# GpSimd's long element-wise instructions in a streaming GLA and differential-attention step, issued as several short ones

## The chip, the cores and the metric

One core of one Trainium2 chip. The time is that of one launch of the kernel in microseconds of the device, the median of several runs. In the profile PE is TensorE's matmuls and PEld its weight loads, DVE is VectorE, ACT is ScalarE, POOL is GpSimd, and SP is the queue from which this kernel issues its DMAs. A name with a q behind it (SPq, POOLq) is an engine's sequencer, which issues in program order.

## What is computed

One layer of a streaming encoder for 1024 new frames of one stream (the "prompt") and 32 frames of a running one (the "sample"), model width 1024, all in 32-bit floats. A projection makes eleven pieces of the normed input; gated linear attention (GLA, 4 heads) and differential attention (8 heads) run beside each other; a merge joins them.

```python
u = rmsnorm(x, pre_norm_g) @ w_in          # split into gq gk gv gr gg dq dk dv dg ma mb
log_a = log_sigmoid(gr @ gla_w_a2 + gla_b_a) / 16
dq, dk = rope(dq, pos), rope(dk, pos)      # the first 16 of each half head's 64 columns
# GLA, in chunks of 64 frames, per head; b = cumsum(log_a)
o = (q * exp(b)) @ state + masked(q k^T exp(b_t - b_s)) @ v
state = exp(b_last) * state + (k * exp(b_last - b))^T @ v
# differential attention, per head, blockwise causal mask
attn = softmax(q1 k1^T / 8) - lam * softmax(q2 k2^T / 8)
o_diff = attn @ v
# merge
yg = rmsnorm(o_gla, gla_norm_g) * silu(gg)
yd = rmsnorm(o_diff, diff_subln_g) * (1 - lambda_init) * silu(dg)
merged = sigmoid(ma) * (yg @ w_proj_gla) + sigmoid(mb) * (yd @ w_proj_diff)
y = x + rmsnorm(merged @ w_out, post_norm_g)
```

The outputs are `y` for both streams, the rotated k rows, the v rows and the GLA states.

## The kernel before

Matmuls of full accuracy are built from pairs. Every operand is split into a high part, which is the number rounded to the matmul's type, and a low part, which is the number minus its high part; three matmuls then make a product (high by high, low weight by high, high weight by low). The splits cost one copy on ACT (the high part) and one subtraction on DVE or POOL (the low part).

The work runs in four stages. In the first (to some 225 us) the input is normed, split into `X` and multiplied with the value weights; the order of PE, ACT, DVE and POOL is written out by hand there. In the second (to some 570 us) the four GLA heads run, in the third (to some 1187 us) the eight heads of differential attention, and in the fourth the output projections and the merge. In the second and third stage a planner (`Order`) writes out PE's order ahead of time: it takes steps of the attention as they become due and fills the time between them with jobs of projection. The other engines' order comes from a scheduler.

A **fill job** multiplies all of `X` with one block of 128 columns of the input weights: three chunks of 352 frames, eight k-steps each, three matmuls a step (L461 `wh` by high, L462 `wl` by high, L463 `wh` by low). Its weights come from `wtile` (L424 to 432): a DMA loads `wr` (L427; there is one buffer of it), ACT makes `wh` (L429), POOL makes `wl` (L431, 128 partitions by 1024 columns, one instruction). They are asked for one job ahead. There are 72 such jobs. Since `wr` has one buffer, the load for the next job waits on SP until ACT and POOL have read the last one, and SP's later DMAs stand behind that load.

POOL also makes these: the low part of the GLA heads' values in `load_v` (L646, 128x512, five for each head, the fifth 32x256 for the sample); the product `sw * stb` of the rotation in `rot_job` (L796, 128x1056, for q and k of eight heads): `rr` is the projection, four DMAs (L794, L795) bring its rotated rows to `sw`, DVE multiplies `rr` with `ct` in three parts (L798) and adds `sw` in three parts (L800), and then `split_q` or `split_k` makes the pairs (L810 to L814, L829 to L832; DMAs at L835 bring k's halves to other partitions); the low part of the values of differential attention in `diff_main` (L909, 128x1024, one for each of eight heads); the power −1/2 in `rsqrt_mean` (L162), and small copies (L238, L847).

Lines of DVE that the prediction names: the scans of a GLA head's gates (L520), its q and k pairs (L540 to L545), its gated output (L718, which reads PSUM `ps_y`; SP stores the result to `ygd` at L721), the gating of a differential head (L861), the evacuations with SiLU (L474), the splits of attention weights (L930) and the sample's parts (L1005, L1021). L225 and L260 are stage 1's low parts of `X` and of the value weights, L213 the matmul that spreads the norm.

Of the kernel before, what the change touches and what calls it, by code (L numbers as in the profile page):

```python
# [11 lines left out]
F32 = mybir.dt.float32  # L12
# [3 lines left out]
ALU = mybir.AluOpType  # L16
# [9 lines left out]
KT = D // P  # L26
# [3 lines left out]
NQ = NP // P  # L30
# [92 lines left out]
def hybrid_step_kernel(ctx: ExitStack, tc: tile.TileContext, a):  # L123
    nc = tc.nc
# [6 lines left out]
    def pool(name, bufs=1, **kw):  # L131
        return tc.alloc_tile_pool(name=name, bufs=bufs, **kw)
# [12 lines left out]
    def tbank(name):  # L145
        return pp.tile([P, 512], F32, tag="t", name=name)

    def obank(name):
        return pp.tile([P, 512], F32, tag="o", name=name)
# [5 lines left out]
    ve.memset(eps, EPS)  # L155
    mhalf = cst.tile([P, 4], F32, name="mhalf")
    nc.gpsimd.memset(mhalf, -0.5)

    def rsqrt_mean(s, w, n, cnt):

        ve.tensor_scalar(s[0:w, 0:n], s[0:w, 0:n], 1.0 / cnt, EPS, op0=ALU.mult, op1=ALU.add)
        nc.gpsimd.tensor_tensor(s[0:w, 0:n], s[0:w, 0:n], mhalf[0:w, 0:n], op=ALU.pow)  # L162
# [262 lines left out]
    def wtile(b):  # L425
        wr = wp.tile([P, KT, P], F32, tag="wr", bufs=1, name="wr")
        dma(wr, a["w128"][b])  # L427
        wh = wp.tile([P, KT, P], F32R, tag="wh", name="wh")
        act(wh, wr, AF.Copy)  # L429
        wl = wp.tile([P, KT, P], F32R, tag="wl", name="wl")  # L430
        nc.gpsimd.tensor_tensor(wl, wr, wh.bitcast(F32), op=ALU.subtract)  # L431
        return wh, wl

    def proj(w, src, evac):
# [170 lines left out]
    def gla_head(h):  # L605
# [3 lines left out]
        for r, c in ((P, slice(0, 8)), (NS, slice(8, 9))):  # L609
            w = P if r == P else NS  # L610
# [27 lines left out]
        def load_v(pr):  # L638
            n, w = (2, P) if pr < 4 else (1, NS)
            vr = tp.tile([P, 2, GDV], F32, tag="vr", name="vr")  # L640
            vh = gp.tile([P, 2, GDV], F32R, tag="vh", bufs=2, name="vh")
            vl = gp.tile([P, 2, GDV], F32R, tag="vl", bufs=2, name="vl")
            dma(vr[0:w, 0:n, :], gvd[pr * 2 * P : pr * 2 * P + n * w, h * GDV : (h + 1) * GDV]
                .rearrange("(c p) e -> p c e", p=w))
            act(vh[0:w, 0:n], vr[0:w, 0:n], AF.Copy)  # L645
            nc.gpsimd.tensor_tensor(vl[0:w, 0:n], vr[0:w, 0:n], vh[0:w, 0:n].bitcast(F32), op=ALU.subtract)  # L646
            S.mark(("v", h, pr))
            vq[pr] = vh, vl

        load_v(4)  # L650
        for grp in (2, 0, 1):
            cs = range(grp * 4, grp * 4 + 4) if grp < 2 else range(8, 9)
            n, w = len(cs), P if grp < 2 else NS
# [12 lines left out]
            for c in cs:  # L666
# [5 lines left out]
                vh, vl = vq[c // 2]  # L672
                vh, vl = vh[0:w, c % 2, :], vl[0:w, c % 2, :]
# [86 lines left out]
    stb = dp.tile([P, T], F32, name="stb")  # L760
    dma(stb, a["ropes"])
    sw = dp.tile([P, T], F32, name="sw")
# [19 lines left out]
    def parts(n, cnt):  # L782

        return [slice(i * n // cnt, (i + 1) * n // cnt) for i in range(cnt)]
    SC = HD ** -0.5

    def rot_job(b, event, needs, split):
        def begin():
            r = dp.tile([P, T], F32, tag="rr", name="rr")

            def done():
                for m in range(2):
                    o = m * HD
                    dma(sw[o : o + 8], r[o + 8 : o + 16])  # L794
                    dma(sw[o + 8 : o + 16], r[o : o + 8])  # L795
                nc.gpsimd.tensor_tensor(sw, sw, stb, op=ALU.mult)  # L796
                for c in parts(T, N["rr"]):
                    ve.tensor_tensor(r[:, c], r[:, c], ct[:, c], op=ALU.mult)  # L798
                for c in parts(T, N["rr"]):
                    ve.tensor_tensor(r[:, c], r[:, c], sw[:, c], op=ALU.add)  # L800
                split(r)
            return (lambda ps, sl: act(r[:, sl], ps, AF.Copy)), done
        return b, event, begin, needs
# [47 lines left out]
    def diff_fin(h, osb, sqo):  # L851
        for n0 in (0, 512):
            yield 0.86, [(("pv", h, 3), W["pv"])], ["o"]
            ps = obank("ps_m")
            mm(ps, one_h, sqo[:, n0 : n0 + 512], start=True, stop=True)
            act(sqo[0:1, n0 : n0 + 512], ps[0:1], AF.Copy)
            S.free("o", W["m_o"])
        st(msd[h : h + 1, :], sqo[0:1, :])
        yield 0.0, [(("dg", h), 0.0)], []
        for c in parts(NP, N["fin"]):  # L860
            ve.scalar_tensor_tensor(osb[:, c], osb[:, c], gs_half, dsg[h][:, c], op0=ALU.mult, op1=ALU.mult)  # L861
        st(ydd[h, :, 0:NP], osb)
        S.mark(("fin", h))
# [32 lines left out]
    def diff_main():  # L896
        fin = None
        for h in range(DH):
            att = {}
            yield 0.0, [(("dq", h), 0.0), (("dk", h), 0.0)], []  # L900
            yield from diff_scores(h, 0, att)
            if fin is not None:
                yield from fin
            vr = tp.tile([P, NQ, P], F32, tag="sg1", name="vr")
            dma(vr, a["newv"][0:NP, h * P : h * P + P].rearrange("(c p) e -> p c e", p=P))
            vh = dp.tile([P, NQ, P], F32R, tag="vh", name="vh")
            vl = dp.tile([P, NQ, P], F32R, tag="vl", name="vl")
            act(vh, vr, AF.Copy)
            nc.gpsimd.tensor_tensor(vl, vr, vh.bitcast(F32), op=ALU.subtract)  # L909
            S.mark(("dv", h))  # L910
            osb = tp.tile([P, NP], F32, tag="o", name="osb")
            sqo = rp.tile([P, NP], F32, tag="gst", name="sqo")
            for i in range(NQ):
                g = i // 2
                if i + 1 < NQ:
                    yield from diff_scores(h, i + 1, att)
                p, lat = att.pop(i)
                if i % 2 == 0:
                    ah = dp.tile([P, NQ, 256], F32R, tag="ah", name="ah")
                    al = dp.tile([P, NQ, 256], F32R, tag="al", name="al")  # L920
                dsl = slice((i % 2) * P, (i % 2) * P + P)
                for j0 in range(0, i + 1, 4):
                    nj = min(4, i + 1 - j0)
                    yield 0.11 * nj, [(("p", h, i), lat)], ["t"]
                    ps = tbank("ps_t")
                    for j in range(j0, j0 + nj):
                        nc.tensor.transpose(ps[:, (j - j0) * P : (j - j0 + 1) * P], p[:, j * P : j * P + P], ident)  # L927
                    pv = ps[:, : nj * P].rearrange("p (c s) -> p c s", s=P)
                    act(ah[:, j0 : j0 + nj, dsl], pv, AF.Copy)  # L929
                    ve.tensor_tensor(al[:, j0 : j0 + nj, dsl], pv, ah[:, j0 : j0 + nj, dsl].bitcast(F32),  # L930
                                     op=ALU.subtract)
                    S.free("t", W["tr_t"])
                S.mark(("at", h, i))
                if i % 2 == 0:
                    continue
                yield 0.32 * (i + 0.5), [(("at", h, i), W["at"]), (("dv", h), W["dv"])], ["o"]
                po = obank("po")[:, 0:256]
                for j in range(i + 1):
                    cs = slice(0, 256) if j < i else slice(P, 256)
                    mm(po[:, cs], vh[:, j, :], ah[:, j, cs], start=(j == 0), stop=False)  # L940
                    mm(po[:, cs], vh[:, j, :], al[:, j, cs], start=False, stop=False)  # L941
                    mm(po[:, cs], vl[:, j, :], ah[:, j, cs], start=False, stop=(j == i))  # L942
                act(sqo[:, g * 256 : g * 256 + 256], po, AF.Square)
                act(osb[:, g * 256 : g * 256 + 256], po, AF.Copy)
                S.free("o", W["pv_o"])
                S.mark(("pv", h, g))
            fin = diff_fin(h, osb, sqo)
        yield from fin
# [85 lines left out]
    for h in range(-1, DH):  # L1034
        need = [(("qk", h - 1), 0.0)] if h >= 1 else []
        n = GATES_DIFF[h + 1]
# [8 lines left out]
    with tc.manual_schedule(engines=PE):  # L1045
        left = S.run(left + [[diff_main(), None, first], [sample_thread(), None, nullcontext],
                             [fill(jobs, xs), None, nullcontext]],
                     until=lambda: ("pv", DH - 1, 3) in S.at and jobs[-1][1] in S.at)
# [110 lines left out]
    for u in range(4):  # L1159
        wr = cp.tile([P, KT, 256], F32, tag="cwr", name="cwr")  # L1160
        dma(wr, a["wout"][u])
        if u == 0:
            wh = cp.tile([P, KT, 256], F32R, tag="cwh", name="cwh")
            wl = cp.tile([P, KT, 256], F32R, tag="cwl", name="cwl")
        else:
            wh, wl = (C[:, n, 0 : KT * 256].rearrange("p (k n) -> p k n", k=KT) for n in (2 * u - 2, 2 * u - 1))
# [6 lines left out]
    op = pool("op", reuse_waits="tile")  # L1173
# [6 lines left out]
    for u in range(4):  # L1180
        wh, wl = cw[u]
        csl = slice(u * 256, u * 256 + 256)
        for i in range(NQ + 1):
            t0 = i * P
            w = P if i < NQ else NS
# [111 lines left out]
```

## Time and profile before

| | |
|---|---|
| median of 3 runs | 1486.08 us (1483.74 to 1489.56) |
| the profiled execution's own time | 1489.96 us |
| its span | 1488.2 us |
| granted clock of TensorE, mean | 0.989 |
| PEld (weight loads) busy | 1330.4 us, 89% of the span |
| DVE busy | 790.4 us, 53% |
| ACT busy | 600.5 us, 40% |
| DMA traffic | 156.58 MB, 105 GB/s over the span |

A row of a timeline reads: start, duration (us from the start of the span), engine, line, operation, output from inputs, shape, count; in brackets how long the engine had been idle before it, and what ended that. A row of groups has the total busy time and the mean ns of one behind the first bar, then the idle time of the engine just ahead of such instructions with what ended it. A row of waits has the waiting engine and line, what it waited for, and then the total, the number of times and the longest. POOL is busy for a fifth of the span, in 186 instructions.

### The profile page before, as it was taken

The numbers are of one execution on the slowest core, as the hardware profiler recorded it, in microseconds if no ns is written. First come the engines' busy times: TensorE is split into PE (matmuls) and PEld (weight loads), VectorE is DVE, ScalarE is ACT, GpSimd is POOL, SyncE is SP. The second block draws the span as 40 slices with busy tenths as digits, with TensorE's granted clock in tenths as the row PEclk, the third lists the DMA queues.
The fourth block names the chain that finished last, engine by engine and source line by source line (L and its number), as shares of the span: only waits on it lengthen the run. The fifth ranks groups of instructions, "written<-read, shape, count | busy, mean of one in ns | idle before, by whom it ended". The sixth has DMA issues, their size and how long they took to land.

```text
span 1488.2 us, 22365 instructions
## 1 busy us (share of the span) xinstructions
PE 1427.6 (96%) x8848; PEld 1330.4 (89%) x8848; DVE 790.4 (53%) x1464; ACT 600.5 (40%) x1262; POOL 298.4 (20%) x186
## 2 busy tenths in 40 slices
PE   8999999998989999899999999999899899999997
PEld 6787778988989899899989998999799789999997
DVE  5612004565565443576767676768665536455415
ACT  4522114445444233355555555555454432221311
POOL 1200002132312133222222322222221111121001
PEclk9999999999999999999999999999999999999999
DMA  8621111122222134313141323233322278643205
GB/s 295 215 99 38 44 43 45 52 74 70 75 89 66 66 101 124 102 47 119 52 115 62 108 74 105 64 100 85 97 62 86 91 264 311 215 135 127 100 1 191
DMA packets 66742, 156.58 MB, mean 105 GB/s; under 512 B 10008, under 2 KB 28568, under 8 KB 65600
## 3 DMA queue, kind: packets, MB, share of 16 engines
q1 hardware_dynamic: 66624, 155.01, 32.2%
q8 instruction: 74, 1.21, 0.3%
q14 instruction: 44, 0.36, 0.1%
HBM read 104.39 MB, written 40.04 MB: 97 GB/s over the span
## 4 chain that ended last, share of the span: by engine, by line
PE 51%; DVE 5%; DMA 4%; ACT 2%; issue 1%; POOL 1%; SPq 0%; DVEq 0%; POOLq 0%; ACTq 0%
PE ps_w L461 9%; PE ps_w L462 9%; PE ps_w L463 9%; PE ps_w L440 2%; PE ps_w L439 2%; PE ps_w L441 2%; PE ps_c L1189 2%; PE ps_c L1191 2%; PE ps_c L1190 2%; PE ps_s L880 2%; PE ps_t L927 2%; PE ps_s L879 2%; DMA ydr<-ydd 1%; PE po L941 1%; PE po L942 1%
## 5 line engine op out<-in xcount | busy, mean ns | idle before, releaser
L461 PE MATMUL ps_w<-X,wh 128*128 128x352 f32 x1344 | 451.8, 336 | 8.4 <-ACT k L492 3.2
L462 PE MATMUL ps_w<-X,wl 128*128 128x352 f32 x1344 | 437.4, 325 | 0.0
L463 PE MATMUL ps_w<-X,wh 128*128 128x352 f32 x1344 | 435.5, 324 | 0.0
L431 POOL TENSOR_TENSOR wl<-wr,wh 128x1024 fp32r<-128x1024 f32 x72 | 178.5, 2479 | 659.6 <-ACT wh L429 535.9
L461 PEld LDWEIGHTS ps_w<-X,wh 128*128 128x128 f32 x1344 | 255.3, 190 | 13.5 <-issue 4.8
L462 PEld LDWEIGHTS ps_w<-X,wl 128*128 128x128 f32 x1344 | 255.3, 190 | 1.2 <-issue 1.2
L463 PEld LDWEIGHTS ps_w<-X,wh 128*128 128x128 f32 x1344 | 256.0, 190 | 0.0
L885 ACT ACTIVATE p<-ps_s,nm 128x256 f32<-128x256 f32 (+7 forms) x128 | 94.6, 741 | 58.7 <-DVE ps_s L881 31.0
L286 PE MATMUL ps_v<-wh,X 128*128 128x512 f32 x248 | 98.1, 396 | 1.9 <-DVE X L225 1.9
L285 PE MATMUL ps_v<-wh,X 128*128 128x512 f32 x248 | 99.5, 401 | 0.0
L287 PE MATMUL ps_v<-wl,X 128*128 128x512 f32 x248 | 98.9, 399 | 0.0
L429 ACT ACTIVATE wh<-wr 128x1024 fp32r<-128x1024 f32 x72 | 75.8, 1053 | 55.1 <-PE ps_w L463 30.4
L883 DVE TENSOR_REDUCE nm<-ps_s 128x1 f32<-128x256 f32 (+7 forms) x128 | 94.7, 746 | 2.7
L272 DVE TENSOR_TENSOR vo<-ps_v,vo 32x512 f32<-32x512 f32 x4 | 2.7, 678 | 141.7 <-ACT vo L271 141.7
L881 DVE MEMSET ps_s<- 64x64 f32 x128 | 14.3, 112 | 114.7 <-PE ps_s L880 113.1
L646 POOL TENSOR_TENSOR vl<-vr,vh 128x512 fp32r<-128x512 f32 (+1 forms) x20 | 24.8, 1238 | 223.9 <-ACT vh L645 223.9
L879 PE MATMUL ps_s<-k,q 128*128 128x512 f32 (+2 forms) x192 | 68.0, 362 | 1.2 <-DMA k<-k 1.2
L880 PE MATMUL ps_s<-kl,q 128*128 128x512 f32 (+2 forms) x192 | 63.9, 348 | 3.7 <-DMA kl<-kl 3.2
L268 ACT ACTIVATE vo<-ps_v 128x512 f32<-128x512 f32 x32 | 19.1, 596 | 116.5 <-PE ps_v L287 115.6
L929 ACT ACTIVATE ah<-ps_t 128x512 fp32r<-128x512 f32 (+2 forms) x96 | 46.9, 488 | 43.8 <-PE ps_t L927 43.1
L930 DVE TENSOR_TENSOR al<-ps_t,ah 128x512 fp32r<-128x512 f32 (+2 forms) x96 | 53.1, 553 | 18.7 <-ACT ah L929 17.4
L440 PE MATMUL ps_w<-Y,wl 128*128 128x352 f32 x192 | 62.3, 324 | 0.0
(319 smaller groups left out, 2971.0 us busy)
## 6 DMA issues: line engine op xcount, KB each, us to landing
wr<-w SPq DMA_DIRECT2D x72, 512.0 KB
thd<-gate SPq DMA_DIRECT2D x16, 528.0 KB
xn<-xn SPq DMA_DIRECT2D x16, 512.0 KB
wr<-wv SPq DMA_DIRECT2D x16, 512.0 KB
newk<-rr SPq DMA_DIRECT2D x8, 528.0 KB
ygr<-ygd SPq DMA_DIRECT2D x8, 528.0 KB
tha<-thd SPq DMA_DIRECT2D x8, 528.0 KB
ydr<-ydd SPq DMA_DIRECT2D x8, 528.0 KB
```

Of the source, the lines that this page charges most:

```text
L285: mm(ps, xk[:, 0, t0 : t0 + P], wh[:, k, :], start=(k == 0), stop=False)
L286: mm(ps, xk[:, 1, t0 : t0 + P], wh[:, k, :], start=False, stop=False)
L287: mm(ps, xk[:, 0, t0 : t0 + P], wl[:, k, :], start=False, stop=(k == KT - 1))
L431: nc.gpsimd.tensor_tensor(wl, wr, wh.bitcast(F32), op=ALU.subtract)
L440: mm(ps[:, :n], wl[:, k, :], src[k][:, 0, t0 : t0 + n], start=False, stop=False)
L461: mm(ps[:, :n], wh[:, k, :], src[k][:, 0, t0 : t0 + n], start=(k == 0), stop=False)
L462: mm(ps[:, :n], wl[:, k, :], src[k][:, 0, t0 : t0 + n], start=False, stop=False)
L463: mm(ps[:, :n], wh[:, k, :], src[k][:, 1, t0 : t0 + n], start=False, stop=(k == KT - 1))
L879: mm(ps[:, n0 : n0 + n], qs[m][:, qsl], ks[m][:, n0 : n0 + n], start=True, stop=False)
L880: mm(ps[:, n0 : n0 + n], qs[m][:, qsl], kls[m][:, n0 : n0 + n], start=False, stop=True)
L883: ve.tensor_reduce(nm, ps[:, 0:w], axis=AX.X, op=ALU.max, negate=True)
L885: act(p[:, 0:w], ps[:, 0:w], AF.Exp, bias=nm, accum_out=sm[:, m : m + 1])
```

## The change

A helper, `gp_tensor`, issues a `tensor_tensor` on POOL as `cnt` instructions, each on an equal share of the second dimension. Four places use it: `wl` in eight pieces of 128x128 (72 jobs), the value pairs of the GLA heads in two pieces of 128x256 (one for the sample's 32x256), the rotation's product in eight pieces of 128x132, and the value pairs of differential attention in eight pieces of 128x128. POOL's instructions grow by 688 (72 and 16 and 8 times seven, and 16 times one). What is computed stays the same.

```diff
+    def gp_tensor(out, in0, in1, op, cnt):
+
+        n = out.shape[1] // cnt
+        for i in range(cnt):
+            c = slice(i * n, i * n + n)
+            nc.gpsimd.tensor_tensor(out[:, c], in0[:, c], in1[:, c], op=op)
...
-        nc.gpsimd.tensor_tensor(wl, wr, wh.bitcast(F32), op=ALU.subtract)
+        gp_tensor(wl, wr, wh.bitcast(F32), ALU.subtract, KT)
...
-            nc.gpsimd.tensor_tensor(vl[0:w, 0:n], vr[0:w, 0:n], vh[0:w, 0:n].bitcast(F32), op=ALU.subtract)
+            gp_tensor(vl[0:w, 0:n], vr[0:w, 0:n], vh[0:w, 0:n].bitcast(F32), ALU.subtract, n)
...
-                nc.gpsimd.tensor_tensor(sw, sw, stb, op=ALU.mult)
+                gp_tensor(sw, sw, stb, ALU.mult, 8)
...
-            nc.gpsimd.tensor_tensor(vl, vr, vh.bitcast(F32), op=ALU.subtract)
+            gp_tensor(vl, vr, vh.bitcast(F32), ALU.subtract, NQ)
```

The order of instructions on PE, DVE, ACT and SP stays as it is; lines behind the helper are seven higher, and all pieces stand on the helper's line, L164. POOL's own order changes little beside the splitting. This is POOL around the branch of the third GLA head and behind it (`fl` is the flag of the branch, `ss` the norm of the head's sample rows); in the trace of before the `wl` behind the branch runs at 438.31. Before:

```order
L162 TENSOR_TENSOR ss<-ss,mhalf 128x4
L431 TENSOR_TENSOR wl<-wr,wh 128x1024 x2
L574 TENSOR_LOAD fl
L575 COMPARE_AND_BRANCH
L575 UNCONDITIONAL_BRANCH x2
L431 TENSOR_TENSOR wl<-wr,wh 128x1024
L646 TENSOR_TENSOR vl<-vr,vh 128x512
L162 TENSOR_TENSOR ss<-ss,mhalf 32x1
L431 TENSOR_TENSOR wl<-wr,wh 128x1024
```

The same place on POOL after the change:

```order
L169 TENSOR_TENSOR ss<-ss,mhalf 128x4
L164 TENSOR_TENSOR wl<-wr,wh 128x128 x14
L581 TENSOR_LOAD fl
L582 COMPARE_AND_BRANCH
L582 UNCONDITIONAL_BRANCH x2
L164 TENSOR_TENSOR wl<-wr,wh 128x128 x10
L164 TENSOR_TENSOR vl<-vr,vh 128x256 x2
L169 TENSOR_TENSOR ss<-ss,mhalf 32x1
L164 TENSOR_TENSOR wl<-wr,wh 128x128 x8
```

Each subtraction is a run of pieces, and the last two pieces of the `wl` ahead of the branch now stand behind it.

The second place is POOL in the third differential head, where the rotation's product, the weights and the values follow one another (`smp` and the 64x1 `ss` belong to the sample's rows); the values run at 750.74 in the trace of before. Before:

```order
L847 COPY smp<-sg 128x32
L431 TENSOR_TENSOR wl<-wr,wh 128x1024
L909 TENSOR_TENSOR vl<-vr,vh 128x1024
L431 TENSOR_TENSOR wl<-wr,wh 128x1024
L162 TENSOR_TENSOR ss<-ss,mhalf 64x1
L796 TENSOR_TENSOR sw<-sw,stb 128x1056
```

After the change POOL has there:

```order
L854 COPY smp<-sg 128x32
L164 TENSOR_TENSOR wl<-wr,wh 128x128 x8
L164 TENSOR_TENSOR vl<-vr,vh 128x128 x8
L164 TENSOR_TENSOR wl<-wr,wh 128x128 x8
L169 TENSOR_TENSOR ss<-ss,mhalf 64x1
L164 TENSOR_TENSOR sw<-sw,stb 128x132 x8
```

The sequence is the same, with eight instructions for each long one.

The third place is PE at the start of a fill job in the first GLA head, with the semaphores that each matmul waits for (`pf` belongs to the head's flag). Before:

```order
L525 MATMUL pf<-ident,fm 1x128 [waits DVE_49]
L461 MATMUL ps_w<-X_88,wh 128x352 [waits Activation_49]
L462 MATMUL ps_w<-X_88,wl 128x352 [waits Pool_49]
L463 MATMUL ps_w<-X_88,wh 128x352
L461 MATMUL ps_w<-X_88,wh 128x352
L462 MATMUL ps_w<-X_88,wl 128x352
L463 MATMUL ps_w<-X_88,wh 128x352
```

The same matmuls on PE after the change:

```order
L532 MATMUL pf<-ident,fm 1x128 [waits DVE_49]
L468 MATMUL ps_w<-X_88,wh 128x352 [waits Activation_49]
L469 MATMUL ps_w<-X_88,wl 128x352 [waits Pool_49]
L470 MATMUL ps_w<-X_88,wh 128x352
L468 MATMUL ps_w<-X_88,wh 128x352
L469 MATMUL ps_w<-X_88,wl 128x352 [waits Pool_49]
L470 MATMUL ps_w<-X_88,wh 128x352
```

In the first chunk each matmul on `wl` now waits for its own piece, where only the first one waited for all of it. PE's rows with a wait for POOL grow from 102 to 594.

## The prediction

> **What bounds the kernel now.** I read the page's busy line first.
>
> ```profile
> PE 1427.6 (96%) x8848; PEld 1330.4 (89%) x8848; DVE 790.4 (53%) x1464; ACT 600.5 (40%) x1262; POOL 298.4 (20%) x186
> ```
>
> The span is 1488.2 us, so PE stands idle for 1488.2 − 1427.6 = 60.6 us; the change leaves PE's own work alone, so all it can move lies in these 60.6. Next come PE's waits: engine and line, what ended the wait, then us in total, times, and the longest.
>
> ```profile
> PE ps_t L927 <- DVE al L930: 4.1, 3, 1.4
> PE ps_y L715 <- DVE yt L718: 3.9, 3, 2.6
> PE ps_st L1002 <- DVE smp L1005: 3.6, 2, 2.3
> PE ps_s L880 <- DMA kl<-kl: 3.2, 3, 2.2
> PE ps_w L461 <- ACT k L492: 3.2, 1, 3.2
> PE po L696 <- DVE o_sb L705: 3.1, 5, 0.9
> PE ps_w L461 <- DVE sg L474: 3.0, 2, 1.9
> PE ps_kt L629 <- DVE k L621: 2.1, 2, 1.3
> ...
> PE ps_n L213 <- POOL ssx L162: 1.8, 2, 1.3
> ```
>
> No row of the list waits for `wl` or for either `vl`: POOL's subtractions are not what PE waits for. Most rows name DVE. So the question is what POOL's long instructions do to DVE, and to the queues behind them. POOL's groups, with their mean ns behind the comma:
>
> ```profile
> L431 POOL TENSOR_TENSOR wl<-wr,wh 128x1024 fp32r<-128x1024 f32 x72 | 178.5, 2479 | 659.6 <-ACT wh L429 535.9 <-PE ps_t L927 55.8 <-ACTq L575 37.6
> L796 POOL TENSOR_TENSOR sw<-sw,stb 128x1056 f32<-128x1056 f32 x16 | 40.8, 2553 | 13.4 <-DMA sw<-rr 10.3 <-DVE sg L474 1.8 <-DVE sm L888 1.2
> L646 POOL TENSOR_TENSOR vl<-vr,vh 128x512 fp32r<-128x512 f32 x16 | 21.8, 1365 | 49.2 <-ACT vh L645 49.2
> ...
> L238 POOL CAST xsm<-X 128x64 fp32r<-128x64 f32 x8 | 1.5, 238 | 4.2 <-DVE X L225 4.2
> ```
>
> **The price of a piece.** No row shows a 128x128 subtraction on POOL. Its bounds come from the undisturbed medians (minimum/median/maximum ns) and from the one place where POOL runs eight short instructions in a row.
>
> ```profile
> L431 POOL TENSOR_TENSOR wl<-wr,wh x72: 2344/2403/3341, 25.2 to 1360.7; 128x1024 fp32r<-128x1024 f32 x72
> L646 POOL TENSOR_TENSOR vl<-vr,vh x20: 726/1292/1862, 230.8 to 542.2; 128x512 fp32r<-128x512 f32 x16, 32x256 fp32r<-32x256 f32 x4
> ...
> 65.77 1.49 POOL L238 CAST xsm<-X 128x64 fp32r<-128x64 f32 x8 [4.25 <-DVE X L225]
> ```
>
> (2403 − 1292) / 512 = 2.17 ns for each column, which leaves 2403 − 1024 × 2.17 = 181 ns fixed. A piece alone is 128 × 2.17 + 181 = 459 ns. The eight casts take 238 ns each but follow one another every (1.49 − 0.24) / 7 = 0.18 us, so 0.06 us of the fixed part overlaps. I take 0.40 us a piece, **3.3 us for eight** where one took 2.40: +0.9. The bounds are 2.40 (all of the fixed part overlaps: +0) and 8 × 0.459 = 3.67 (none: +1.27). The Trainium skill ("GPSIMD Engine Reference", section 3.1) gives 4497 ns for 2048 columns; by it the fixed part would be an estimated 53 ns, eight pieces some 2.65 us, and the sum below about 2 us lower. The trace's 181 ns disagrees and decides.
>
> Lateness of `wl` itself costs nothing: each is made one job ahead. The tightest place I found is this one, a subtraction and the first matmul on it:
>
> ```profile
> 1214.81 2.40 POOL L431 TENSOR_TENSOR wl<-wr,wh 128x1024 fp32r<-128x1024 f32 x1 [29.34 <-ACT wh L429]
> ...
> 1218.83 0.32 PE L462 MATMUL ps_w<-y,wl 128*128 128x352 f32 x1
> ```
>
> 1.62 us lie between; piece k is asked for only k × 0.48 us later, so +0.9 still fits, and so does +1.27. The added waits of PE, one for each piece, are then met before they are asked; I take 0 for them. A bound from above: all of PE's idle time, 60.6 us over 8848 matmuls, is 0.007 us each, so some 490 more waits are under 3.4 us.
>
> Three short runs change places on POOL: a power now stands between two halves of `vl`, six of eight pieces of one `wl` stand ahead of a branch and two behind it (twice), and a copy of `smp` stands inside a run of `wl`. Each moves something by at most a few pieces, 1 us, against a job of 72 matmuls at 1427.6 / 8848 = 0.16 us, 11.6 us, by which `wl` is ahead: 0; the bound is the 1.62 above.
>
> **What is gained: DVE gets in earlier.** These rows are of POOL and DVE at one place, and of the PE wait behind it.
>
> ```profile
> 438.31 2.51 POOL L431 TENSOR_TENSOR wl<-wr,wh 128x1024 fp32r<-128x1024 f32 x1 [14.54 <-ACT wh L429]
> 440.79 1.40 POOL L646 TENSOR_TENSOR vl<-vr,vh 128x512 fp32r<-128x512 f32 x1
> ...
> 438.56 2.55 DVE L520 TENSOR_TENSOR_SCAN b<-ones,t 128x128 f32<-128x128 f32 x1
> 441.03 1.45 DVE L520 TENSOR_TENSOR_SCAN b<-ones,t 128x128 f32<-128x128 f32 x1
> 446.38 0.43 PE L461 MATMUL ps_w<-X,wh 128*128 128x352 f32 x1 [1.90 <-DVE sg L474]
> ```
>
> A scan takes 0.4 us, but this one stands until 441.11, 0.29 us after POOL's instruction ends; the next one stands until 442.48, when POOL's second ends. Between POOL's two, the first scan did get in. So DVE is let in where one POOL instruction ends, even if the next is ready. With pieces, a held DVE instruction waits for a piece, not for eight. The four scans would alternate with pieces at some 0.5 us each and end near 440.6 instead of 442.8: 2.2 us earlier, more than PE's 1.9. Gain **1.9**. At the other places:
>
> ```profile
> L861 DVE SCALAR_TENSOR_TENSOR osb<-osb,gs_half,sg x8: 1286/2979/3004, 682.0 to 1188.1; 128x1024 f32<-128x1024 f32 x8
> L545 DVE TENSOR_TENSOR kl<-t,kh x4: 2098/2221/2231, 257.8 to 488.1; 128x1056 fp32r<-128x1056 f32 x4
> L543 DVE TENSOR_TENSOR t<-k,t x4: 1257/1258/1258, 255.4 to 485.6; 128x1056 f32<-128x1056 f32 x4
> ```
>
> - L861 takes 1.29 free and 2.98 at the median, held by POOL's `vl` (L909). It stands ahead of `smp` (L1005) in both L1002 waits (3.6 us, the shorter 1.3): 1.4 earlier each, capped by 1.3, gives **2.7**.
> - L545 takes 2.22 where L543 of the same size takes 1.26, held by `wl`. Two of its four stand ahead of L718 and a PE wait of 0.6 (3.9 − 2.6 over the other two): **1.2**.
> - L927, L492, L629 (4.1 + 3.2 + 2.1 us) and a few waits of 0.4 (0.8) sum to 10.2. Held DVE instructions are among those ahead of each, seldom the last one. I take a quarter, **2.6**; the bounds are 0 and 10.2.
>
> Sum of the gains: 8.4.
>
> **What is lost: what stands behind POOL's last piece.** SP's queue issues in order, and its load of the next weights waits until POOL has read the old ones:
>
> ```profile
> SPq L427 <- POOL wl L431: 187.2, 56, 14.7
> ...
> 387.25 2.51 POOL L431 TENSOR_TENSOR wl<-wr,wh 128x1024 fp32r<-128x1024 f32 x1 [4.50 <-ACT wh L429]
> 388.78 2.09 DVE L542 TENSOR_TENSOR ql<-t,qh 128x1056 fp32r<-128x1056 f32 x1
> 389.78 0.34 SPq L427 DMA_DIRECT2D wr<-w  x1
> 390.22 0.38 SPq L721 DMA_DIRECT2D ygd<-yt  x1
> 394.63 0.75 DVE L718 SCALAR_TENSOR_TENSOR yt<-ps_y,gg_half,sg 128x512 f32<-128x512 f32 x1 [1.73 <-DMA ygd<-yt]
> 396.10 0.38 PE L696 MATMUL po<-vh,ah 128*128 128x256 f32 x1 [0.86 <-DVE o_sb L705]
> ```
>
> The load goes out when POOL ends (389.76). The store of `ygd` behind it frees `yt`, L718 waits for that, and PE waits for the copy behind L718. After the change POOL needs 3.3 us, and L542 (I take 1.1 us by itself, a little under the 1.26 of L543, which is of its size), which today stands until POOL is done, gets in between two pieces and holds POOL in turn. POOL ends near 387.25 + 3.3 + 1.1 = 391.65: the store and PE are **1.9** later. Of the five waits at L696 in PE's list three stand behind such a store, one in each of three heads: 3 × 1.9 = 5.7. Bounds for one: 0.9 if DVE holds nothing up, 2.3 with the price at its upper bound.
>
> In stage 1 the chain `wl`, then the power for `ssx`, then the broadcast `ps_n` is on PE's path:
>
> ```profile
> 50.82 2.39 POOL L431 TENSOR_TENSOR wl<-wr,wh 128x1024 fp32r<-128x1024 f32 x1 [3.58 <-ACT wh L429]
> ...
> 54.51 1.46 POOL L162 TENSOR_TENSOR ssx<-ssx,mhalf 128x1 f32<-128x1 f32 x1 [1.29 <-DVE ssx L161]
> ...
> 56.02 0.58 PE L213 MATMUL ps_n<-ident,ssx 128*128 128x128 f32 x1 [0.52 <-POOL ssx L162]
> ```
>
> Eight pieces, with two DVE subtractions of 1.1 us together let in between, end near 55.2, and the power, behind a DVE instruction of 1.2, near 56.9 instead of 55.97: **1.0**. Losses: 6.7. Bounds: 3.0 and 8.
>
> **Sum.** −8.4 + 6.7 = −1.7 us. The profiled execution took 1489.96 (span 1488.2 and 1.76 around it); it would take 1488.3. It lies 3.9 above the median of three, 1486.08, within the runs' own spread of 1483.74 to 1489.56, and the sum is a difference, so I set it against the median: **1484.4**. A difference under 0.5% (7.4 us) is about what a measurement of this kernel can tell from none.
>
> **The rivals.** *The queue price isn't paid.* If POOL's pieces cost nothing extra and the stores behind them don't move, the 8.4 stand alone, and up to 7.6 more where I took a quarter: 1470 to 1478, near 1476. For it: 60.6 us of idle with DVE named in most rows. Against it: the in-order queue above. Chance 0.23.
>
> *The lock isn't given back between pieces.* A queued piece might take it again before DVE does. Then a held instruction waits 3.3 instead of 2.4 at nine places: 9 × 0.9 + 6.7 = +14.8, about 1501. The scan at 438.56 speaks against it, though it got in where POOL's next instruction was of another tile. Chance 0.06. The Trainium skill ("SBUF — State Buffer", section "Who interferes with whom") calls the shared port pair an exclusive lock, which the first to start holds; the trace agrees that DVE stands, 2.55 us for a scan of 0.4. It doesn't say who is next when pieces are queued; by a lock that queued pieces keep, it would be this rival.
>
> *The rotation becomes late (slower).* The product `sw` is on the way to k, and PE already waits for `kl` (3.2 us, three times).
>
> ```profile
> 914.73 2.44 POOL L796 TENSOR_TENSOR sw<-sw,stb 128x1056 f32<-128x1056 f32 x1
> ...
> 917.18 0.94 DVE L798 TENSOR_TENSOR rr<-rr,ct 128x352 f32<-128x352 f32 x2
> ```
>
> The additions (L800) come after three products with `ct` of 0.47, 1.4 us after `sw` ends here, so +0.9 is hidden. It decides from 1.4 on: at 0.46 a piece, with DVE's products let in between, `sw` takes 2.44 + 1.27 + 0.5 and eight heads pay up to 1.27 each: −1.7 + 10.2 = +8.5, about 1495. Chance 0.11.
>
> *It doesn't do what it says.* `load_v` is cut in two only, or one. If short pieces were merged on POOL, nothing would change: 1486. The order of instructions speaks against that: 0.03.
>
> **How the numbers follow.** The forecast has what is left, 0.57, and its own range is 1478.7 to 1490 (gains of 5.8 to 10.4 against losses of 3 to 8 give 1478.7 to 1488.3, and the runs' spread some 2 more above). The range of all is 1475 to 1497: it leaves out the far part of the first rival (0.08) and of the two slower ones (0.08). Faster 0.23; within 0.5% 0.57 + 0.03 = 0.60; slower 0.06 + 0.11 = 0.17.
>
> **What would show it.** Pieces 0.40 us apart, POOL busy for some 380 us instead of 298; scans at 438 of under 0.6 each and the 446.38 wait gone; L861 near 1.6; L696's wait over 5 us. I am wrong if a piece is under 0.33 or over 0.46 us, if DVE stands through more than one piece, or if `ygd` goes out as before.

## The result, and the profile after

The changed kernel takes **1503.74 us**, the median of four runs (1501.04 to 1505.80), where the kernel before takes 1486.00 (four runs, 1483.74 to 1489.56): a ratio of 1.0109, with a 95% interval of 1.0083 to 1.0135. The forecast of 1484.4, with its range of 1475 to 1497, was wrong, and in sign too. The profiled execution took 1504.61 us, with a span of 1502.9.

The page's line of busy times, of the kernel after:

```profile
PE 1434.4 (95%) x8848; PEld 1339.1 (89%) x8848; DVE 741.5 (49%) x1464; ACT 600.1 (40%) x1262; POOL 439.8 (29%) x874
```

PE's waits in the same kernel (total us, times, longest):

```profile
PE po L703 <- DVE o_sb L712: 10.3, 4, 3.3
PE ps_w L468 <- DVE tha L1085: 4.3, 5, 1.8
PE ps_a L561 <- DVE yt L725: 4.1, 2, 2.1
...
PE ps_w L468 <- DVE sg L481: 1.1, 1, 1.1
PE ps_st L1009 <- DVE smp L1012: 0.8, 1, 0.8
```

DVE is busy for 49 us less: it stands less behind POOL, as meant. The waits for `sg` (3.0 before) and `smp` (3.6 before) shrank as forecast. But the wait at `po` (L696 before, L703 now) grew from 3.1 to 10.3, and two rows are new or larger: `ps_a` for `yt`, and `ps_w` for `tha` (0.8 before). PE's busy time itself grew by 6.8 us.

Both traces hold the same 8848 matmuls in the same order, so the delay of each against its twin can be read off, and summed by the time in the trace of before:

| stretch of the kernel before | gained or lost after the change |
|---|---|
| 0 to 200 us (stage 1) | +0.4 |
| 200 to 300 (first GLA head) | −2.9 |
| 300 to 500 (GLA heads) | **+17.3** |
| 500 to 1050 (differential heads) | −6.0 |
| 1050 to 1200 | +0.7 |
| 1200 to 1300 (projections, merge) | **+3.8** |
| behind the last matmul | +1.4 |

The sum is the 14.7 us between the two spans. The medians lie 17.7 apart: the profiled execution of before took 4.0 us more than its median, that of after 0.9 more. This is the place in the GLA heads that the prediction worked out, from the timeline after: POOL's weights, DVE, SP, DVE, and PE.

```profile
390.90 4.73 POOL L164 TENSOR_TENSOR wl<-wr,wh 128x128 fp32r<-128x128 f32 x8 [3.79 <-ACT wh L436]
392.43 1.42 DVE L549 TENSOR_TENSOR ql<-t,qh 128x1056 fp32r<-128x1056 f32 x1
395.65 0.35 SPq L434 DMA_DIRECT2D wr<-w  x1
396.09 5.38 SPq L728 DMA_DIRECT2D ygd<-yt  x2
400.37 0.75 DVE L725 SCALAR_TENSOR_TENSOR yt<-ps_y,gg_half,sg 128x512 f32<-128x512 f32 x1 [4.35 <-DMA ygd<-yt]
401.85 0.58 PE L703 MATMUL po<-vh,ah 128*128 128x256 f32 x1 [3.23 <-DVE o_sb L712]
```

The chain is the forecast one. `wl` takes 4.73 us from its first piece to its last where it took 2.51. SP's load goes out when it ends, `ygd` behind the load, and PE stands for 3.23 us instead of 0.86. The next `wl` of the same head does it again, at a place that the prediction didn't look at:

```profile
412.59 4.53 POOL L164 TENSOR_TENSOR wl<-wr,wh 128x128 fp32r<-128x128 f32 x8 [2.56 <-ACT wh L436]
417.15 0.33 SPq L434 DMA_DIRECT2D wr<-w  x1
422.05 0.75 DVE L725 SCALAR_TENSOR_TENSOR yt<-ps_y,gg_half,sg 128x512 f32<-128x512 f32 x1 [5.84 <-DMA ygd<-yt]
422.86 0.33 PE L561 MATMUL ps_a<-qh,kh 128*128 128x128 f32 x1 [2.06 <-DVE yt L725]
```

The same place in the kernel before:

```profile
405.41 2.52 POOL L431 TENSOR_TENSOR wl<-wr,wh 128x1024 fp32r<-128x1024 f32 x1 [2.51 <-ACT wh L429]
407.96 0.33 SPq L427 DMA_DIRECT2D wr<-w  x1
409.74 3.75 SPq L721 DMA_DIRECT2D ygd<-yt  x2
```

There the load left 1.8 us ahead of the store of `ygd`, which waited for DVE alone. Now the load is what the store waits for.

In the merge it is the loads of `ydr` (L1062 before) that come late. These rows are again of the kernel after:

```profile
1266.28 4.40 POOL L164 TENSOR_TENSOR wl<-wr,wh 128x128 fp32r<-128x128 f32 x8 [9.42 <-ACT wh L436]
1270.70 0.33 SPq L434 DMA_DIRECT2D wr<-w  x1
1271.79 0.32 SPq L1143 DMA_DIRECT2D rsb<-rsd  x1
1272.96 1.92 SPq L1069 DMA_DIRECT2D ydr<-ydd  x2
1268.88 2.88 DVE L1144 TENSOR_TENSOR ydr<-ydr,rsb 128x1024 f32<-128x1024 f32 x2 [3.35 <-DMA ydr<-ydd]
1282.88 2.49 DVE L1144 TENSOR_TENSOR ydr<-ydr,rsb 128x1024 f32<-128x1024 f32 x2 [4.78 <-DMA ydr<-ydd]
1287.03 0.43 PE L468 MATMUL ps_w<-y,wh 128*128 128x352 f32 x1 [1.81 <-DVE tha L1085]
```

DVE's scaling waits 4.78 us for the loads of `ydr`, and DVE is late for PE. But the load of weights isn't what holds them at this place: it leaves 1.1 us ahead of SP's next instruction, `rsb`, and that one leaves 0.03 us after DVE's last scaling ended (1271.76). The loads of `ydr` are used 9.9 us after the first is issued (1272.96 to 1282.88), where 6.6 stood in the kernel before (1249.22 to 1255.85). Why they land later isn't shown by these rows.

Of the 17.3 us in the GLA heads only some 8.0 are changes of a wait by over 0.4 us. The rest is PE's pace. These are windows of PE: the stretch, its length, PE's busy time and count, and then the granted clock. The first six rows are of the kernel after.

```profile
325.50:333.50 8.00, 7.99 (x40) 0.57 0.33 99
326.45:333.27 6.82, 6.82 (x33) 0.50 0.25 76
343.51:346.93 3.42, 3.42 (x14) 0.50 0.21 77
401.54:404.95 3.41, 3.10 (x13) 0.50 0.52 154
486.87:490.29 3.42, 3.42 (x14) 0.50 0.55 153
507.35:514.18 6.83, 6.83 (x30) 0.50 0.10 38
```

And two of the kernel before; the first is the same work as the first row above:

```profile
326.00:334.00 8.00, 7.49 (x60) 1.00 0.37 115
...
506.40:509.80 3.40, 3.40 (x13) 0.50 0.50 157
```

The first row reaches a little past its stretch; cut to the stretches, the clock is one half, for 3.41 or 6.83 us: 40 matmuls in 8 us where 60 ran before. Half of the 23.9 us of the five stretches is 12.0; read by twins, their matmuls lost 10.7. Gaps that changed by less than 0.4 us give back 1.4, and the three make the 17.3. Four of the stretches stand behind waits that the change made longer (`po` three times, `ps_a` once). The one at 343.51 stands behind a wait of 2.65 us that the kernel before has too, at 340.51, and without a loss of clock there.

Outside these heads the kernel before has more of it: from 200 to 1450 us its stretches at half clock last 17.1 us and those of the kernel after 34.1, so 8.5 us were lost by the clock over the whole kernel. The mean clock of the other executions agrees: 0.980 to 0.984 in the four of the changed kernel, 0.988 to 0.995 in 52 of the kernel before.

### The profile page after: what moved, and what is told of

It is laid out like the page before. It is cut to its first block, busy times and chain, and to the rows that moved or that the text cites. A ratio compares the mean times of both kernels' runs of the same rounds, so it can differ in the third digit from the quotient of the medians.

```text
span 1502.9 us, 23109 instructions
## 1 busy us (share of the span) xinstructions
PE 1434.4 (95%) x8848; PEld 1339.1 (89%) x8848; DVE 741.5 (49%) x1464; ACT 600.1 (40%) x1262; POOL 439.8 (29%) x874
## 5 line engine op out<-in xcount | busy, mean ns | idle before, releaser
L164 POOL TENSOR_TENSOR wl<-wr,wh 128x128 fp32r<-128x128 f32 x576 | 278.5, 519 | 582.8 <-ACT wh L436 464.2
L164 POOL TENSOR_TENSOR vl<-vr,vh 128x128 fp32r<-128x128 f32 (+2 forms) x100 | 63.1, 661 | 244.0 <-ACT vh L652 219.1
L164 POOL TENSOR_TENSOR sw<-sw,stb 128x132 f32<-128x132 f32 x128 | 64.7, 540 | 2.7 <-DMA sw<-rr 1.9
L937 DVE TENSOR_TENSOR al<-ps_t,ah 128x512 fp32r<-128x512 f32 (+2 forms) x96 | 53.1, 553 | 18.7 <-ACT ah L936 17.3
```

The lines of the kernel that those rows point to most:

```text
L164: nc.gpsimd.tensor_tensor(out[:, c], in0[:, c], in1[:, c], op=op)
```

## The experiments

Two theories were set against each other at first. **Q**: the loss is `wl`'s later end, handed on by SP's order. **N**: the loss is the price of 688 more instructions and 492 more waits. A third, **R**, blames the rotation's product and the values.

**Only the weights in pieces** (`e1_only_wl`): the other three places whole.

```diff
-            gp_tensor(vl[0:w, 0:n], vr[0:w, 0:n], vh[0:w, 0:n].bitcast(F32), ALU.subtract, n)
+            nc.gpsimd.tensor_tensor(vl[0:w, 0:n], vr[0:w, 0:n], vh[0:w, 0:n].bitcast(F32), op=ALU.subtract)
...
-                gp_tensor(sw, sw, stb, ALU.mult, 8)
+                nc.gpsimd.tensor_tensor(sw, sw, stb, op=ALU.mult)
...
-            gp_tensor(vl, vr, vh.bitcast(F32), ALU.subtract, NQ)
+            nc.gpsimd.tensor_tensor(vl, vr, vh.bitcast(F32), op=ALU.subtract)
```

> Only the weights' subtraction (wl) is in eight pieces; the rotation's product and both value subtractions are whole again. Theory Q (SP's queue: wl ends 0.9 to 2.2 us later, the load of the next weights stands behind it on SP, and the ygd stores and ydr loads behind that; PE then stalls, and runs slowly after the longer stalls): the loss is nearly all here, 1500 to 1506 us, with three waits at the po matmuls of 3.3 us each and two at ps_a of 2.1 as in the changed kernel. Theory R (the loss comes from the rotation's product and the values in pieces): 1484 to 1490. Theory N (490 more waits on PE and 688 more instructions cost by their number): 504 of 688 are here, so about three quarters of the loss, 1499, spread evenly over the span and without those five waits.

Measured: 1505.39 us, ratio 1.0129 (1.0107 to 1.0152). The whole loss is here. Its waits for PE:

```profile
PE po L703 <- DVE o_sb L712: 10.5, 4, 3.5
PE ps_a L561 <- DVE yt L725: 4.1, 2, 2.1
PE ps_st L1009 <- DVE smp L1012: 3.6, 2, 2.3
```

The five long waits are those of the changed kernel, and the wait for `smp` is that of before. R is out.

**All but the weights in pieces** (`e2_all_but_wl`).

```diff
-        gp_tensor(wl, wr, wh.bitcast(F32), ALU.subtract, KT)
+        nc.gpsimd.tensor_tensor(wl, wr, wh.bitcast(F32), op=ALU.subtract)
```

> The rotation's product and both value subtractions are in pieces, wl is whole as before the change. Theory Q: no loss, a small gain where DVE's gating of the differential heads (behind the values) gets in earlier: 1480 to 1487, the waits of ps_st for smp 2 to 3 us shorter in all. Theory R: 1496 to 1504. Theory N: 184 of 688 instructions, about +4: 1490.

Measured: 1487.82 us, ratio 1.0011 (0.9998 to 1.0025), no difference that can be told. The `smp` wait went (−1.4 and −1.5 us at its two places, read by twins), but three waits of the attention came 0.7 to 1.0 us later, behind the rotation's product. The time lies just above Q's range of 1480 to 1487: a gain of some us, which Q forecast, can't be told.

**The loads taken out of SP's queue**, with everything in pieces (`e3_split_poolq`) and with everything whole (`e4_whole_poolq`). POOL issues each load itself, behind its own `wl`.

```diff
+    wjobs = []
...
-        dma(wr, a["w128"][b])
+        (dma if len(wjobs) < 3 else nc.gpsimd.dma_start)(wr, a["w128"][b])
+        wjobs.append(b)
```

> Everything in pieces as in the changed kernel, but the loads of the fill jobs' weights (from the fourth job on) are issued by POOL behind its own wl, so nothing on SP stands behind a wl. Theory Q: the three waits at po and the two at ps_a fall under 1 us each, the waits for tha in the merge too, and the time is 8 us or more under the changed kernel's 1504, at 1478 to 1494. Theory N: the number of pieces and of waits is the same, so it stays at 1500 or more.

> The kernel before the change with the same loads issued by POOL: the control of the run above. Theory Q: 0 to 8 us under 1486, since the stores behind a whole wl wait too (0.9 and 1.0 us stalls at po), and the run above is then no slower than this one by more than 4 us, or faster, as DVE is held for 50 us less. Theory N: the run above is 12 us or more slower than this.

Measured: in pieces 1482.10 us, ratio 0.9968 (0.9950 to 0.9985); whole 1489.96, ratio 1.0015 (1.0001 to 1.0028). This settles Q against N: with the same pieces and the same waits on PE the time falls by 21.6 us, and pieces turn from a loss into a gain of 7.9 against their own control. The place in question, of the run in pieces:

```profile
381.96 4.72 POOL L164 TENSOR_TENSOR wl<-wr,wh 128x128 fp32r<-128x128 f32 x8 [3.12 <-ACT wh L439]
386.98 0.60 POOL L436 DMA_DIRECT2D wr<-w  x1 [0.30 <-PE ps_w L473]
...
383.60 4.16 SPq L731 DMA_DIRECT2D ygd<-yt  x2
```

`wl` takes as long as in the changed kernel (4.72 us), but the store leaves at 383.60, in the midst of it. PE's waits of that run:

```profile
PE po L706 <- DVE o_sb L715: 2.4, 4, 0.9
...
PE ps_w L471 <- DVE tha L1088: 0.9, 2, 0.5
```

The granted clock from 300 to 525 us is 1.00 in this run, where it was 0.95 in the changed kernel. The control is no faster than the kernel before, against Q's 0 to 8 us: in the merge PE's waits for `tha` came to 3.0 us, where 0.8 stood before. That trace took 1498.22 us, 8 us above its kernel's median, so the 3.0 may be high. POOL's issue of a load takes 0.58 us of its time at the median; whether that is the cause was not tried.

For the merge the runs say less than for the GLA heads. The waits for `tha` come to 3.3 us with only the weights in pieces, to 1.1 with all but the weights, to 0.9 with pieces and POOL's loads, but to 3.0 in the control, with every instruction whole. So the pieces of `wl` bring them with the loads on SP, and what else does stays open.

**Fewer pieces** tells where the length of `wl` comes from: from the price of a piece (P), or from DVE's instructions, let in between pieces and holding POOL (L). Only `wl` is split, in two (`e6_wl_in_2`) or four (`e7_wl_in_4`).

```diff
-        gp_tensor(wl, wr, wh.bitcast(F32), ALU.subtract, KT)
+        gp_tensor(wl, wr, wh.bitcast(F32), ALU.subtract, 4)
```

> Only wl is split, in two pieces of 128x512, loads on SP. Theory L (wl ends late mostly because DVE's long instructions get in between pieces and hold POOL for 1.1 to 1.3 us): with the one boundary 1.3 us after the start, and DVE's instruction asking 1.5 us after it, nothing gets in at the three stores; wl ends 0.1 to 0.2 later, the po waits stay at 0.5 to 1.1, and the time is 1484 to 1490. Theory P (only the price of the pieces, 0.9 us for seven boundaries, 0.13 for one): the same here, 1487 to 1490.

> Only wl is split, in four pieces of 128x256, loads on SP. Theory L: three boundaries cost 0.4 us, but the boundary 2.1 us after the start lets DVE's instruction in, so wl ends 1.6 to 1.9 us later at the three stores: po waits of 2.3 to 3.0 us each, time 1495 to 1503. Theory P: wl ends 0.4 later, po waits of 1.2 to 1.7, time 1490 to 1495.

Measured: two pieces 1489.04 us, ratio 1.0016 (1.0004 to 1.0029); four pieces 1501.10, ratio 1.0112 (1.0080 to 1.0143). First two pieces at the place of the store, with DVE's instruction, then four:

```profile
382.38 2.66 POOL L164 TENSOR_TENSOR wl<-wr,wh 128x512 fp32r<-128x512 f32 x2 [4.50 <-ACT wh L436]
383.91 2.24 DVE L549 TENSOR_TENSOR ql<-t,qh 128x1056 fp32r<-128x1056 f32 x1
```

```profile
387.02 3.96 POOL L164 TENSOR_TENSOR wl<-wr,wh 128x256 fp32r<-128x256 f32 x4 [4.50 <-ACT wh L436]
388.56 1.83 DVE L549 TENSOR_TENSOR ql<-t,qh 128x1056 fp32r<-128x1056 f32 x1
```

And the wait at `po` with four:

```profile
PE po L703 <- DVE o_sb L712: 8.1, 4, 2.6
```

With two pieces DVE asks after the one boundary, stands until POOL is done (2.24 us), and POOL takes 2.66. With four it gets in at the third boundary, and POOL takes 3.96, of which four undisturbed pieces are 2.77 (the shortest of the 72 jobs). So of the 1.56 us above a whole one (2.40), 1.2 are DVE's instruction and 0.4 the pieces' price. L holds: the time, 1501.10, and the three waits of 2.5 to 2.6 us at `po` lie in its ranges and above those of P, though `wl` ends 1.5 us later than in the kernel before, a little less than its 1.6 to 1.9. The time of two pieces fits both; one of its `po` waits, 1.5 us, is longer than either expected.

**Pieces only where no store stands behind** (`e8_wl_diff_jobs`): the 24 jobs of the differential heads' q, k and gate.

```diff
-        gp_tensor(wl, wr, wh.bitcast(F32), ALU.subtract, KT)
+        gp_tensor(wl, wr, wh.bitcast(F32), ALU.subtract, KT if BLK_DQ <= b < BLK_MA else 1)
```

> Only wl is split, in eight pieces, and only in the 24 jobs of the differential heads' q, k and gate; the other 48 jobs are whole, loads on SP. Theory Q: the stores of ygd and the loads of ydr stand behind whole wl as before the change, so the loss of the second stage and of the merge is not there: 1482 to 1488, with no po wait over 1.2 us. Theory N (cost by the number of instructions and waits): 168 of 504 instructions, a third of the loss of all jobs in pieces: about 1493.

Measured: 1485.32 us, ratio 0.9989 (0.9977 to 1.0001). A third of the pieces costs nothing, as Q says; one `po` wait of 1.6 us is longer than it expected. Its `wl` is whole, and the store leaves as soon behind it as before; but `yt` comes free 5.2 us after the store is issued (315.78 to 320.96), where 3.9 stood before (320.04 to 323.98). So that wait isn't of the pieces.

**The gain sought** (`e5_poolq_wl_vl`): the run with POOL's own loads, with the first two `wl`, the GLA values and the rotation's product whole.

```diff
-        gp_tensor(wl, wr, wh.bitcast(F32), ALU.subtract, KT)
+        gp_tensor(wl, wr, wh.bitcast(F32), ALU.subtract, 1 if len(wjobs) < 3 else KT)
...
-            gp_tensor(vl[0:w, 0:n], vr[0:w, 0:n], vh[0:w, 0:n].bitcast(F32), ALU.subtract, n)
+            nc.gpsimd.tensor_tensor(vl[0:w, 0:n], vr[0:w, 0:n], vh[0:w, 0:n].bitcast(F32), op=ALU.subtract)
...
-                gp_tensor(sw, sw, stb, ALU.mult, 8)
+                nc.gpsimd.tensor_tensor(sw, sw, stb, op=ALU.mult)
```

> The kernel with the weights' loads on POOL, with three parts made whole again: the first two wl (stage 1), the GLA heads' values and the rotation's product; wl from the third job on and the differential heads' values stay in eight pieces. Theory H (a whole run of eight pieces can keep one DVE instruction waiting through all of it, as the scalar multiplication of the sample's output did behind the rotation's product, 3.48 us against 2.47 for a whole one): the four waits of PE that came 1.0 to 1.1 us later there go, and stage 1's wait for the norm shrinks: 1475 to 1480, 2 to 6 us under the run with everything in pieces. Rival: the product in pieces lets DVE's rotation in earlier and that is worth as much: 1481 to 1486.

Measured: 1481.55 us, ratio 0.9963 (0.9950 to 0.9976), no different from 1482.10 with the product in pieces. Stage 1's wait for the norm fell from 4.3 to 1.8 us, and three waits behind the product went (1.0 each by twins), but others of 0.5 to 1.5 us came in the same heads, so H found its waits and not its gain; the time lies in the rival's range of 1481 to 1486. Both runs beat both kernels: pieces pay once no store or load on SP stands behind their end.

## Why the prediction was wrong

- **A piece**: 3.3 us for eight, forecast from 2.17 ns a column and an overlap of 0.06. The shortest runs of eight take 3.35. Right. But POOL is busy for 439.8 us, not the 380 forecast: the 72 runs take 3.73 at the median and up to 5.42, as DVE gets in between.
- **DVE gets in between pieces**: right. The four scans, which are now these rows, and the gating of a differential head:

```profile
447.02 4.00 POOL L164 TENSOR_TENSOR wl<-wr,wh 128x128 fp32r<-128x128 f32 x8 [11.38 <-ACT wh L436]
446.93 2.03 DVE L527 TENSOR_TENSOR_SCAN b<-ones,t 128x128 f32<-128x128 f32 x4
...
764.00 1.47 DVE L868 SCALAR_TENSOR_TENSOR osb<-osb,gs_half,sg 128x1024 f32<-128x1024 f32 x1 [0.39 <-ACT osb L951]
```

  Four scans in 2.03 us instead of 4.57, and 1.47 instead of 2.97. By twins PE gained 2.1 us behind the scans (1.9 forecast), 2.9 at `smp` (2.7), 1.3 at L715 (1.2). The quarter of the other waits, 2.6, was too much: PE's waits for `al` at `ps_t`, for ACT's `k` and for DVE's `k` fell by 3.2 in all, while those at `ps_t` for `ps_s` and at `ps_so` grew by 2.2. The Trainium skill ("SBUF — State Buffer", section "Who interferes with whom") says that the holder keeps the pair for the whole instruction; the trace agrees, for a piece too.
- **The store behind the load**: the mechanism was right and the size was short. `wl` ends 2.2 us later, not 1.9, and three waits cost 7.6 us, not 5.7. The first of them is 0.4 us in the trace of before and 1.6 in `e8_wl_diff_jobs`, where `wl` is whole too, so up to 1.2 of the 7.6 may be the store's landing.
- **The step that failed** is the count of what stands behind `wl`'s end. I looked for waits that exist in the profile of before, and found three stores. Two more stores of `ygd` stand behind another `wl` (the one shown had 1.8 us to spare), and in the merge the loads of `ydr`, on the same queue as the weights' loads, came late in a way that stays open: 4.3 and 3.8 us that the sum didn't have. At those stores I booked only the gain of 1.2 us from the same job.
- **PE's own time** was taken as fixed ("the change leaves PE's own work alone, so all it can move lies in these 60.6"). It isn't: waits of 2 to 3.4 us were followed by 3.41 or 6.83 us at half the clock, 8.5 us more over the whole kernel than before. This is the largest missing term, and without it the loss between the two traces would have been near 6 us. Some of it is luck, as the stretch at 343.51 shows.
- **Stage 1**: +1.0 forecast; PE came 0.7 us later at the place (56.73 against 56.02), +0.4 is left at 200 us and nothing at 225. Right in its way, and too large. **The rotation's lateness**, the rival on the slower side, did not come: the waits for `kl` are 3.2 and 3.3 us.
- **The range**: its gains stop at 10.4 us, though the bounds of the quarter (0 to 10.2) allow 16.0. The miss lies on the other side.
- **The lock that isn't given back** gave nearly the right time, 1501, for the wrong reason: DVE's standing fell. It was seen in a few cases only, below.

## What to carry to other kernels

Cutting a long instruction lets another engine in, and that makes the cut instruction end later by what was let in: ask what waits for its last piece, over every queue in program order, and not only what waits today, since a store or load with 1.8 us to spare becomes the bound when the end moves by 2.2. Take the dependent transfer out of the shared queue first; the same cut then turned from a loss of 1.1% into a gain of 0.3 to 0.4%. Where PE's clock falls after an idle stretch, a new wait costs more than its length: here the five stretches at half clock in the GLA heads lost 10.7 us behind waits of some 14 us in all.

## What the runs showed of the hardware

- **PE's clock after a wait.** In the traces the granted clock is 1.00 or 0.50 and changes only in steps of 3.41 us: the five falls shown, at 326.45, 343.51, 401.54, 486.87 and 507.35, lie 5, 17, 25 and 6 such steps apart. The length of a wait alone doesn't decide; how long PE idles within one step does. These are two steps of the kernel after around a wait of 2.06 us that ended at 422.86, and the step with the wait of 2.02 that ended at 507.09:

```profile
418.61:422.02 3.41, 2.18 (x14) 1.00 0.58 207
422.02:425.43 3.41, 2.58 (x20) 1.00 0.21 77
...
503.94:507.35 3.41, 1.39 (x10) 1.00 0.44 173
```

  The first wait is cut in two by the border of two steps, and the clock stays full. The second lies within one, and the clock falls in the next (the last of the six rows in the section on the result). In the run with only the weights in pieces the first wait comes again, 2.06 us long, but within one step, and there the clock falls:

```profile
415.50:418.91 3.41, 1.36 (x9) 1.00 0.48 184
418.93:425.73 6.80, 6.80 (x28) 0.50 0.10 39
...
418.92 0.48 PE L561 MATMUL ps_a<-qh,kh 128*128 128x128 f32 x1 [2.06 <-DVE yt L725]
```

  In the ten traces, from 200 to 1440 us, the clock fell behind each of the 44 steps at full clock in which PE idled for more than 1.85 us, behind 8 of the 43 with 1.4 to 1.85, and behind none of the 3477 with less. The steps lie elsewhere against the program in each execution, so the same wait can cost the clock in one and not in the next. Why a fall lasts one step or two stays open. The Trainium skill ("TensorE: Matmul & The Clock Gate", section "Part 1: The HAM clock gate") puts the drop to half behind an idle window of about 3.4 us that runs freely; the drops here agree with half a clock and with steps of 3.41 us, and come behind steps in which PE still worked for up to 2 us.
- **A DVE instruction can stand through a whole run of pieces.** The same scalar multiplication of 64x128 takes 0.28 us free. After the change it came 0.06 us behind the start of the rotation's eight pieces three times:

```profile
779.31 3.46 POOL L164 TENSOR_TENSOR sw<-sw,stb 128x132 f32<-128x132 f32 x8
779.37 3.48 DVE L1028 TENSOR_SCALAR os__8813<-os__8813,ss 64x128 f32<-64x128 f32 x1 [0.66 <-POOL ss L169]
...
925.24 0.57 DVE L1028 TENSOR_SCALAR os__10577<-os__10577,ss 64x128 f32<-64x128 f32 x1 [0.67 <-POOL ss L169]
```

  Twice it was let in only after all eight (3.48 and 3.50 us), once after one. The two other kernels with this product in pieces and the same line showed the same, twice in three. The prediction named this, DVE standing through more than one piece, as a sign that it is wrong. Why it happens stays open.
- **A load issued by POOL** takes 0.58 us of POOL's time, the median of 69 in the run in pieces (0.57 to 1.30).
